# A hybrid attention trunk on one core: the keys of turned weight tiles are written apart by residue modulo four, and values are turned by pairs of columns

## The chip, the cores and the metric

The kernel runs on one core of a Trainium2 chip. The metric is the device time of one execution in microseconds. The engines are named as the profile names them: PE (TensorE: matrix products; PEld is its weight load), ACT (ScalarE), DVE (VectorE), POOL (GpSimd) and SP (SyncE, whose queue issues every DMA of this kernel).

## What is computed

One layer of a streaming encoder on a prompt of 1024 tokens and a sample of 32 tokens, width 1024, with 8 heads of band attention (A) and 8 heads of stick-breaking attention (B), 64 wide each:

```python
qa, ka, va, ga, qb, kb, vb, gb = split(rmsnorm(h, g_pre) @ w_in)     # 8 x 512 columns
# A: each frame sees its own 64-frame chunk and the 8 chunks before
s = qa @ ka.T * 64 ** -0.5 + bias_table[clip(k_pos - q_pos, -128, 128) + 128]
oa = softmax(where(in_band, s, -1e30)) @ va
# B: strictly causal
z = qb @ kb.T * 64 ** -0.5
log_1m = where(causal, log_sigmoid(-z), 0)
after = cumsum(log_1m, reverse=True) - log_1m
ob = where(causal, exp(log_sigmoid(z) + after), 0) @ vb
y = concat(oa * silu(ga), ob * silu(gb)) @ w_out
h = h + rmsnorm(y, g_post)
h = h + sigmoid(h @ w_ple_gate) * (p @ w_ple)
```

Besides the two streams of outputs, the new keys and values of both kinds go out.

## The kernel before

Nothing is issued as it is written. Every call is recorded with its tiles; a planner (`plan`, with the costs of `cost` and the constants at lines 179 to 185) lays the recorded operations out on five engines by list scheduling, sets due times from that layout and lays them out again, three times. The order that comes out is each engine's instruction order, and each engine then runs its own list in order. A change of one cost can therefore move rows on every engine.

The projections run as `col_steps`: for each of 32 groups of 128 columns, three chunks of 352 tokens, 24 products a chunk (`mm_...`), fp32 split into a high and a low part. They are woven with the attention, pair of heads by pair of heads, in the order A0, B0, A1, B1 and so on.

`attention` handles one head. For each block `i` of 128 queries, `scores(i)` makes the scores (`SA`, `SB`), and from them a tile of weights in `be` with 128 queries on the partitions and `n` keys along the row. For A, DVE adds the bias and takes a minimum (`om`, `stat`), and ACT writes the exponential. For B, ACT takes a sigmoid, DVE scans it, and POOL writes the difference of neighbours. Both read `om` (`w0`) and write `be` (`w1`). `weights_t(i)` must bring the keys onto the partitions, since `values(g)` multiplies the weights with the values (`PVA`, `PVB`). It does so in two ways. Small blocks are transposed by PE (`ptw`). The blocks in `ROUND` (A: 4, 5, 6, 7, each alone; B: 4, 5, 6, each alone) are turned without PE: DVE transposes 32 x 32 squares from `be` into `om`, one DMA writes them to a scratch in DRAM (`swap`), a second one reads them back into `be` so that the squares stand on their partitions, ACT casts a high part (`wTh`) and DVE subtracts it for the low part (`wTl`). For the scratch to be written in long runs, a square takes every fourth key: the residue of the key modulo 4 is the slow index.

The values come out of the projection turned the wrong way as well (`st`, 128 features by 1024 tokens). `values_out` transposes them on DVE into `vx`, in squares that take every fourth token, writes them to a scratch with one DMA and reads them back into `st` with another; ACT copies them into `vt`, and they go out and into the operands of the products (`v2`). Keys that go out (`keys_out`, `kt`) are transposed by DVE in plain squares.

All DMAs stand in one SP queue. SP waits, in order, until what a DMA reads is written, so that a DMA that waits holds back all behind it.

Of the kernel before, what the change touches and what calls it, by code (L numbers as in the profile page):

```python
# [10 lines left out]
AF = mybir.ActivationFunctionType  # L11
ALU = mybir.AluOpType

P = 128
D = 1024
# [163 lines left out]
LAND = {"PE": 165, "ACT": 0, "DVE": 0, "POOL": 0, "SP": 0, "CTL": 0}  # L179
SEM = 60  # L180
WAKE = {"PE": 400, "ACT": 100, "DVE": 100, "POOL": 190, "SP": 0}
ISSUE = 520
DMA_RATE, LANDING, WAKE_DMA = 320.0, 2500, 200
TABLE_NS = 1310
DVE_SET, POOL_SET = 137, 110
# [79 lines left out]
class Recorder:  # L265
# [73 lines left out]
    @staticmethod  # L339
    def cost(eng, method, args, kw, writes, reads):  # L340

        out = writes[0] if writes else None
        n = out.free() if isinstance(out, View) else 1
        psum = any(isinstance(v, (View, Segments)) and v.buf.psum for v in reads)
        if eng == "PE":
            if method == "transpose":
                return (109 if args[1].shape[0] > 64 else 62), 165
            return max(109.0, 2.5 + 0.449 * args[2].free()) * (1 if args[2].buf.dtype == F32R else 4), 165
        if eng == "ACT":
            return (90 if psum else 125) + 0.83 * n + (190 if "accum_out" in kw else 0), 105  # L350
        if eng == "DVE":
            if method == "tensor_tensor_scan":
                return 150 + 2.1 * n, 85
            if method == "tensor_copy" and not psum:
                return 100 + 0.53 * n, 85
            if method == "scalar_tensor_tensor":
                return 155 + 1.04 * n, 85
            if method == "tensor_tensor_reduce":
                return 120 + 1.04 * n, 150
            return 100 + 1.04 * n, 85  # L360
        if eng == "POOL":
            if method == "tensor_tensor":
                if n == 1:
                    return 565, 40
                return 200 + (1.77 if out.buf.dtype == F32 else 2.15) * n, 40
            if method == "tensor_scalar":
                return 255 + 0.86 * n, 0
            return 100 + 0.82 * n, 0
        size, run = 4, 0
        for v in (out, args[1]):  # L370
            if isinstance(v, View) and v.buf.pool is not None:
                size, run = 4 * v.shape[0] * v.free(), 4 * v.shape[-1]
        return ISSUE, max(size / DMA_RATE, size / run * (8.5 + 0.0365 * run) / 16)


    def order(self):
# [123 lines left out]
def stream_step(  # L500
# [19 lines left out]
    def scratch(shape, name):  # L520
        return Buf(shape, F32, name=name, real=dram.tile(shape, F32, tag=name, name=name))
# [206 lines left out]
    def values_out(ab, p, src, o_p, o_s, then):  # L728

        h2 = slice(2 * p, 2 * p + 2)  # L730
        b0 = 4 if ab == "A" else 0
        box = {}

        def turn():
            st = src()
            D = scratch([4, P, SEQ // 4], f"swap{ab}{p}")
            x = at2.tile([P, SEQ], F32, tag="tok", name=f"vx{ab}{p}", bufs=2)
            nc.vector.transpose(x.rearrange("p (c b f) -> p b c f", c=4, f=32), st[:, 0:SEQ].rearrange("p (b t c) -> p b c t", c=4, t=32))
            dma(D.rearrange("g (t c) x -> (g t) (c x)", c=4), x)
            dma(st[:, 0:SEQ].rearrange("p (g x) -> p g x", g=4), D.rearrange("g p x -> p g x"))  # L740
            out = at2.tile([P, NT, P], F32, tag="tok", name=f"vt{ab}{p}", bufs=2)
            box["out"] = out
            short_block(st, out, f"ptv{ab}{p}")

        def back():
            out = box["out"]
            nc.scalar.copy(out[:, 0:8, :].rearrange("p b (g f) -> p g b f", g=4), src()[:, 0:SEQ].rearrange("p (g b f) -> p g b f", g=4, f=32))
            dma(o_p[0, 0, :, h2, :].rearrange("(b p) h d -> p b (h d)", p=P), out[:, b0:8, :])
            dma(o_s[0, 0, :, h2, :].rearrange("p h d -> p (h d)"), out[0:NS, 8, :])
            then(out)  # L750

        return [(0.1, turn), (0.0, back)]
# [79 lines left out]
    def attention(ab, p, h):  # L832
# [23 lines left out]
        def rooms(i):  # L856
# [8 lines left out]
            w0, w1 = whole[g]  # L865
            return w0[:, a + more * k:a + more * k + n + more], w1[:, a:a + n]

        def scores(i):
            L, kd, kl = Lq[h], KDh[h], KLD[h]
            b0 = lo_block(i)  # L870
            n = (i + 1 - b0) * P
            k0 = b0 * P
            cut = [0, n] if n <= 512 else [0, n // 2, n]
            w0, w1 = rooms(i)
            pieces = []
            for j in range(len(cut) - 1):
                s = psum("S", f"S{nm}_{i}_{j}")[:, 0:cut[j + 1] - cut[j]]
                lhs = L[:, i * P:(i + 1) * P]
                ks = slice(k0 + cut[j], k0 + cut[j + 1])
                nc.tensor.matmul(s, lhs, kd[:, ks], start=True, stop=False)  # L880
                nc.tensor.matmul(s, lhs, kl[:, ks], start=False, stop=True)
                pieces.append((cut[j], cut[j + 1], s))
            if ab == "B":
                a, b, s = pieces[-1]
                dg = s[:, b - a - P:b - a]
                nc.vector.tensor_tensor(dg, dg, maskb, ALU.add)
                nc.gpsimd.memset(w0[:, n:n + 1], 1.0)
                for a, b, s in pieces:
                    nc.scalar.activation(w0[:, a:b], s, AF.Sigmoid, scale=-1.0)
                for a, b, s in reversed(pieces):  # L890
                    rev = w0[:, a:b][:, ::-1]
                    nc.vector.tensor_tensor_scan(rev, rev, s, w0[:, b:b + 1], ALU.mult, ALU.bypass)
                nc.gpsimd.tensor_tensor(w1[:, 0:n], w0[:, 1:n + 1], w0[:, 0:n], ALU.subtract)
            else:
                m = small.tile([P, 4], F32, tag="stat", name=f"stat{nm}_{i}", bufs=6)
                sums = box["sums"]
                for j, (a, b, s) in enumerate(pieces):
                    nc.vector.tensor_tensor_reduce(
                        w0[:, a:b], s, box["bias"][:, n - b:n - a][:, ::-1], 1.0,
                        3e38 if j == 0 else m[:, j - 1:j], ALU.add, ALU.min, m[:, j:j + 1])  # L900
                last = len(pieces) - 1
                nc.scalar.activation(w1[:, 0:n], w0[:, 0:n], AF.Exp, bias=m[:, last:last + 1], scale=-1.0, accum_out=sums[:, i:i + 1])
                if i == 7:
                    nc.vector.reciprocal(sums, sums)
                    pt = psum("T", f"pts{nm}")
                    nc.tensor.transpose(pt[0:8, 0:P], sums, ident)
                    row = at.tile([P, 4 * P], F32, tag="ot", name=f"sumrow{nm}", bufs=2)[0:8, 0:P]
                    nc.scalar.copy(row, pt[0:8, 0:P])
                    dma(rs_dr[2 * p + h, 0:SEQ].rearrange("(i q) -> i q", q=P), row)
            state[i] = w0, w1  # L910
# [7 lines left out]
        def weights_t(i):  # L918
# [9 lines left out]
            if i in together:  # L928

                group = together[i]  # L930
                done_with.append((i, hi, lo))
                if i != group[-1]:
                    return
                w0, w1 = whole[group]
                m = sum(cost(x) for x in group)
                first = {x: sum(cost(y) for y in group[:k]) for k, x in enumerate(group)}
                squares = w0[:, 0:m * P].rearrange("p (c b q) -> p b c q", c=4, q=32)
                for x, _, _ in done_with:
                    y = slice(first[x], first[x] + cost(x))
                    nc.vector.transpose(squares[:, y], w1[:, y.start * P:y.stop * P].rearrange("p (b k c) -> p b c k", c=4, k=32))  # L940
                dr = scratch([4, P, m * 32], f"swap{nm}_{i}")
                dma(dr.rearrange("g (k c) x -> (g k) (c x)", c=4), w0[:, 0:m * P])
                dma(w1.rearrange("p (g x) -> p g x", g=4), dr.rearrange("g p x -> p g x"))
                turned = w1.rearrange("p (g b q) -> p g b q", g=4, q=32)
                for x, hi, lo in done_with:
                    src = turned[:, :, first[x]:first[x] + cost(x), :]
                    hi, lo = (y.rearrange("p (b g q) -> p g b q", g=4, q=32) for y in (hi, lo))
                    nc.scalar.copy(hi, src)
                    nc.vector.tensor_tensor(lo, src, f(hi), ALU.subtract)
                done_with.clear()  # L950
                return
# [955 lines left out]
```

## Time and profile before

| | |
|---|---|
| median of 3 runs | 796.02 us (794.12 to 798.11) |
| profiled execution | 797.65 us, with a span of 795.9 us in the trace |
| busy over the span | PE 97%, PEld 89%, DVE 78%, ACT 63%, POOL 55% |
| DMA | 177.83 MB, mean 223 GB/s |

Nearly every instruction has the line of the planner's `emit`, L494, so groups are read by tile names: `om<-be` is the turning transposition, `be<-om,statA` the exponential of A, `be<-om` on POOL the difference of B. A group's row has its count, its busy time in us, the mean of one in ns, and the idle time of the engine before it. In the stretches, the clock of 1.00 is TensorE at full speed. PE counts as busy while a product is under way, and products overlap, so short pauses do not show.

### The profile page before, as it was taken

How to read it: one execution, taken by the hardware profiler on the slowest of the kernel's cores; microseconds unless marked ns; L12 is line 12 of the kernel's file. 1: busy time of each engine (PE TensorE's matmuls, PEld its weight loads, DVE VectorE, ACT ScalarE, POOL GpSimd, SP SyncE). 2: the span in 40 equal slices, each digit the busy share in tenths (PEclk: the TensorE clock that was granted, in tenths of full speed). 3: DMA queues.
4: the chain of work that ended last, by engine and by line, in shares of the span. 5: the costliest groups of instructions: out<-in, count | busy, mean ns of one | idle time of the engine just before them, and what ended most of it. 6: DMA issues, size and time to landing. Idle time of an engine off the chain costs nothing.

```text
span 795.9 us, 13838 instructions
## 1 busy us (share of the span) xinstructions
PE 775.4 (97%) x4518; PEld 710.2 (89%) x4518; DVE 622.2 (78%) x1007; ACT 502.9 (63%) x1039; POOL 438.3 (55%) x503
## 2 busy tenths in 40 slices
PE   8999999999999899999999999999999999999997
PEld 7999998999999799999899989999997877888786
DVE  6716799899899789999899799986446778676655
ACT  5736685577686546886567686542349967874841
POOL 4714647773556668145552426867634358596613
PEclk9999999999999999999999999999999999999999
DMA  8519996777998749876446859865679848668634
GB/s 269 162 39 287 286 296 232 210 251 276 274 273 271 208 153 324 232 206 209 122 137 214 206 162 292 264 191 165 196 259 340 288 133 271 225 213 288 252 127 133
DMA packets 175179, 177.83 MB, mean 223 GB/s; under 512 B 38002, under 2 KB 131930, under 8 KB 175107
## 3 DMA queue, kind: packets, MB, share of 16 engines
q1 hardware_dynamic: 175106, 176.95, 72.4%
q8 instruction: 36, 0.59, 0.3%
q14 instruction: 37, 0.30, 0.1%
HBM read 107.62 MB, written 60.88 MB: 212 GB/s over the span
## 4 chain that ended last, share of the span: by engine, by line
PE 41%; DVE 8%; issue 2%; DMA 2%; ACT 1%; POOL 0%; SPq 0%; DVEq 0%; ACTq 0%; POOLq 0%
PE mm_gB L494 6%; PE mm_gA L494 4%; DVE om L494 3%; PE g0P L494 2%; PE o1P L494 2%; PE g1P L494 2%; PE g2P L494 2%; PE o0P L494 2%; PE g3P L494 2%; PE o3P L494 2%; PE o2P L494 2%; PE ple L494 2%; PE PVB L494 2%; PE mm_vA L494 1%; DVE wTl L494 1%
## 5 line engine op out<-in xcount | busy, mean ns | idle before, releaser
L494 POOL TENSOR_TENSOR be<-om 128x384 f32<-128x384 f32 (+7 forms) x64 | 79.4, 1248 | 56.9 <-DVE om L494 19.7
L494 DVE TENSOR_TENSOR_SCAN om<-om,SB 128x384 f32<-128x384 f32 (+5 forms) x96 | 94.6, 998 | 5.5 <-DMA sum_drg<-gB 2.5
L494 DVE STREAM_TRANSPOSE om<-be 128x640 f32<-128x640 f32 (+2 forms) x56 | 79.8, 1433 | 3.8 <-POOL be L494 3.2
L494 DVE TENSOR_TENSOR wTl<-be,wTh 128x640 fp32r<-128x640 f32 (+2 forms) x56 | 58.6, 1050 | 10.3 <-ACT wTh L494 10.1
L494 ACT ACTIVATE om<-SB 128x384 f32<-128x384 f32 (+5 forms) x96 | 44.2, 491 | 32.8 <-DVE SB L494 13.7
L494 ACT CAST wTh<-be 128x640 fp32r<-128x640 f32 (+2 forms) x56 | 43.1, 771 | 17.7 <-DMA be<-swapB 12.5
L494 ACT ACTIVATE be<-om,statA 128x640 f32<-128x640 f32 (+4 forms) x64 | 44.4, 695 | 9.3 <-DVE statA L494 5.1
L494 PE MATMUL SB<-kdB,LB 128*128 128x384 f32 (+5 forms) x96 | 33.7, 354 | 2.3 <-DVE om L494 2.2
L494 POOL TENSOR_TENSOR oB<-oB,oB 128x256 f32<-128x256 f32 x32 | 24.1, 777 | 20.1 <-DMA oB<-in_w_out_dram 19.9
L494 DVE CUSTOM_DVE_ANT_0 om<-SA,biasA 128x320 f32<-128x320 f32 (+3 forms) x64 | 29.8, 482 | 6.8 <-PE SA L494 4.8
L494 ACT CAST wTh<-ptwB 128x512 fp32r<-128x512 f32 (+3 forms) x48 | 22.3, 483 | 17.7 <-PE ptwB L494 11.2
L494 PE MATMUL SB<-klB,LB 128*128 128x384 f32 (+5 forms) x96 | 33.1, 348 | 0.0
L494 POOL TENSOR_TENSOR gB<-gB,gB 128x256 f32<-128x256 f32 x32 | 25.5, 821 | 10.6 <-DMA gB<-in_w_ple_gate_dram 9.1
L494 PE MATMUL SA<-klA,LA 128*128 128x320 f32 (+2 forms) x96 | 29.4, 317 | 0.5 <-DMA klA<-klA 0.5
L494 PE MATMUL SA<-kdA,LA 128*128 128x320 f32 (+2 forms) x96 | 29.5, 317 | 0.3 <-DVE statA L494 0.3
L494 POOL TENSOR_TENSOR sggA<-sggA,oggA 128x352 f32<-128x352 f32 x24 | 23.9, 994 | 7.5 <-DMA oggA<-rs_dr 3.7
L494 POOL TENSOR_TENSOR klB<-stkB,kdB 64x1024 fp32r<-64x1024 f32 x8 | 20.4, 2548 | 13.7 <-ACT kdB L494 9.3
L494 DVE TENSOR_TENSOR wTl<-ptwB,wTh 128x512 fp32r<-128x512 f32 (+3 forms) x48 | 25.4, 542 | 3.1 <-ACT wTh L494 1.6
L494 PE MATMUL PVB<-wTh,v2B 128*128 128x512 f32 (+1 forms) x96 | 22.2, 354 | 3.2 <-ACT wTh L494 2.4
L494 POOL TENSOR_TENSOR h<-h,x 128x512 f32<-128x512 f32 (+1 forms) x18 | 23.9, 1350 | 0.0
L494 PEld LDWEIGHTS PVB<-wTh,v2B 128*128 128x128 f32 x96 | 17.6, 193 | 7.1 <-ACT wTh L494 3.3
L494 POOL TENSOR_TENSOR klA<-stkA,kdA 64x1024 fp32r<-64x1024 f32 x8 | 19.5, 2438 | 7.6 <-ACT kdA L494 7.4
(707 smaller groups left out, 2627.4 us busy)
## 6 DMA issues: line engine op xcount, KB each, us to landing
swapA<-om SPq DMA_DIRECT2D x32, 320.0 KB
be<-swapA SPq DMA_DIRECT2D x32, 320.0 KB
oB<-in_w_out_dram SPq DMA_DIRECT2D x16, 256.0 KB
sum_dro<-oB SPq DMA_DIRECT2D x16, 256.0 KB
gB<-in_w_ple_gate_dram SPq DMA_DIRECT2D x16, 256.0 KB
sum_drg<-gB SPq DMA_DIRECT2D x16, 256.0 KB
x<-in_x_prompt_dram SPq DMA_DIRECT2D x16, 256.0 KB
h_dr<-h SPq DMA_DIRECT2D x8, 512.0 KB
```

Of the source, the lines that this page charges most:

```text
L494: getattr(getattr(tc.nc, o.what[0]), o.what[1])(*args, **kw)
```

## The change

Three edits. First, `apart` gives the round's tiles a permuted view of `be`: ACT's exponential and POOL's difference read `om` in order as before, and write key `4k + c` of each block of 128 to place `32c + k`, that is, neighbouring keys 32 floats (128 bytes) apart. DVE's transposition then reads `be` with unit step. What lies in `om`, in the scratch and after it is the same as before. Blocks that PE transposes are not touched.

Second, the values' squares take every second token instead of every fourth (a step of 8 bytes in place of 16), and the two halves of 512 tokens lie in separate halves of the scratch. The write has two runs of 2 KB for each partition in place of one of 4 KB; the read back is two DMAs of 64 partitions in place of one of 128.

Third, the planner's costs: one issue cost of 520 ns becomes 470, 610 for tiles of 64 partitions, and 660 for views of three dimensions with 16 or more in the middle; and a transposition that reads a view of four dimensions is costed at 1.98 ns an element, a form that no longer occurs with the first two edits (the values' view has five dimensions).

```diff
-ISSUE = 520
+ISSUE, ISSUE_64, ISSUE_SHORT = 470, 610, 660
...
+            if method == "transpose" and len(args[1].shape) == 4:
+                return 1.98 * n + 30, 85
...
+                issue = ISSUE_64 if v.shape[0] == 64 else ISSUE_SHORT if len(v.shape) == 3 and v.shape[1] >= 16 else ISSUE
...
-            D = scratch([4, P, SEQ // 4], f"swap{ab}{p}")
+            D = scratch([2, 4, HD, SEQ // 4], f"swap{ab}{p}")
             x = at2.tile([P, SEQ], F32, tag="tok", name=f"vx{ab}{p}", bufs=2)
-            nc.vector.transpose(x.rearrange("p (c b f) -> p b c f", c=4, f=32), st[:, 0:SEQ].rearrange("p (b t c) -> p b c t", c=4, t=32))
-            dma(D.rearrange("g (t c) x -> (g t) (c x)", c=4), x)
-            dma(st[:, 0:SEQ].rearrange("p (g x) -> p g x", g=4), D.rearrange("g p x -> p g x"))
+            nc.vector.transpose(x.rearrange("p (i j b f) -> p b i j f", i=2, j=2, f=32), st[:, 0:SEQ].rearrange("p (b i t j) -> p b i j t", i=2, t=32, j=2))
+            dma(D.rearrange("i g (t j) x -> (g t) i (j x)", j=2), x.rearrange("p (i x) -> p i x", i=2))
+            for i in range(2):
+                dma(st[HD * i:HD * i + HD, 0:SEQ].rearrange("p (g x) -> p g x", g=4), D[i].rearrange("g p x -> p g x"))
...
+        def apart(i, x, out=False):
+
+            if i not in together:
+                return x
+            return x.rearrange("p (b c k) -> p b k c" if out else "p (b k c) -> p b k c", c=4, k=32)
...
-                nc.gpsimd.tensor_tensor(w1[:, 0:n], w0[:, 1:n + 1], w0[:, 0:n], ALU.subtract)
+                nc.gpsimd.tensor_tensor(apart(i, w1[:, 0:n], True), apart(i, w0[:, 1:n + 1]), apart(i, w0[:, 0:n]), ALU.subtract)
...
-                nc.scalar.activation(w1[:, 0:n], w0[:, 0:n], AF.Exp, bias=m[:, last:last + 1], scale=-1.0, accum_out=sums[:, i:i + 1])
+                nc.scalar.activation(apart(i, w1[:, 0:n], True), apart(i, w0[:, 0:n]), AF.Exp, bias=m[:, last:last + 1], scale=-1.0, accum_out=sums[:, i:i + 1])
...
-                    nc.vector.transpose(squares[:, y], w1[:, y.start * P:y.stop * P].rearrange("p (b k c) -> p b c k", c=4, k=32))
+                    nc.vector.transpose(squares[:, y], w1[:, y.start * P:y.stop * P])
```

The order of rows that the planner makes of it differs on all engines. On SP, the first head's values, before (`stvA0` is read back by one transfer, after the first turned tile's write):

```order
L494 DMA oB110_991<-in_w_out_dram 128x512
L494 DMA klA01_973<-klA01_973 64x1024
L494 DMA swapA00_4_99<-om_189 128x640
L494 DMA stvA0_676<-swapA0_98 128x4x256
L494 DMA out_7_dram<-vtA0_1002 32x128
```

and now:

```order
L497 DMA oB110_981<-in_w_out_dram 128x512
L497 DMA klA01_974<-klA01_974 64x1024
L497 DMA stvA0_676<-swapA0_98 64x4x256 x2
L497 DMA biasA10_1071<-r_dr_76 128x640
L497 DMA swapA00_4_99<-om_189 128x640
```

The read back is two rows of 64 partitions, and it now stands ahead of the first turned tile's write.

More of the change, by code (lines that the diff above doesn't have):

```diff
@@ L368, in cost @@
             return 100 + 0.82 * n, 0
-        size, run = 4, 0
+        size, run, issue = 4, 0, ISSUE
         for v in (out, args[1]):
@@ L372, in cost @@
                 size, run = 4 * v.shape[0] * v.free(), 4 * v.shape[-1]
-        return ISSUE, max(size / DMA_RATE, size / run * (8.5 + 0.0365 * run) / 16)
+                issue = ISSUE_64 if v.shape[0] == 64 else ISSUE_SHORT if len(v.shape) == 3 and v.shape[1] >= 16 else ISSUE
+        return issue, max(size / DMA_RATE, size / run * (8.5 + 0.0365 * run) / 16)
     def order(self):
```

## The prediction

> **What bounds the kernel now.** First the page: the span, and what share of it each engine was busy.
>
> ```profile
> span 795.9 us, 13838 instructions
> PE 775.4 (97%) x4518; PEld 710.2 (89%) x4518; DVE 622.2 (78%) x1007; ACT 502.9 (63%) x1039; POOL 438.3 (55%) x503
> ```
>
> TensorE is busy for 97% of the span, so nothing here can win more than the 20.5 us in which it is not. Where those lie, the busy times by stretch show: the start, the first heads, the attention from 120 to 520 us, the gates, and the two last products. The second fence has the same view in 20 us slices, of which I show five.
>
> ```profile
> 40.00:120.00 80.00, 78.69 (x500) 76.13 (x499) 51.67 (x102) 48.85 (x105) 33.00 (x42) 1.00 0.79 229
> 120.00:520.00 400.00, 389.15 (x2443) 370.51 (x2442) 362.75 (x581) 265.99 (x557) 221.95 (x261) 1.00 0.76 226
> 520.00:600.00 80.00, 80.00 (x504) 78.79 (x503) 45.64 (x73) 30.42 (x63) 48.45 (x51) 1.00 0.63 203
> ```
>
> ```profile
> 140.00:160.00 20.00, 20.00 (x127) 19.22 (x125) 17.61 (x27) 11.42 (x26) 14.95 (x22) 1.00 0.75 211
> 160.00:180.00 20.00, 20.00 (x129) 19.72 (x128) 19.78 (x22) 14.61 (x28) 15.72 (x13) 1.00 0.75 234
> 260.00:280.00 20.00, 17.04 (x96) 15.01 (x94) 15.03 (x20) 11.14 (x25) 13.28 (x18) 0.91 0.72 201
> 280.00:300.00 20.00, 20.00 (x129) 19.10 (x128) 16.60 (x27) 8.59 (x21) 12.98 (x18) 1.00 0.54 171
> 440.00:460.00 20.00, 19.04 (x125) 18.48 (x124) 14.86 (x35) 13.04 (x27) 8.79 (x6) 1.00 0.83 203
> ```
>
> After the length stand the busy times of TensorE, its weight loads, VectorE, ScalarE and GpSimd, then the granted clock. From 40 to 520 us TensorE idles 1.31 + 10.85 = 12.2 us, and 260:280 alone has 3.0 of them and a clock of 0.91 behind them (0.09 x 20 = 1.8 us more). VectorE is the second limit: 362.75 of 400 us, 91%. But a full VectorE is not by itself a waiting TensorE: 160:180 has 19.78 us of VectorE and no idle TensorE, 440:460 has 14.86 and 0.96 us. What TensorE waits for is local, and the view of waits for 40 to 520 us names it:
>
> ```profile
> PE PVB L494 <- ACT wTh L494: 2.4, 3, 1.1
> PE SB L494 <- DVE om L494: 2.2, 4, 0.9
> PE ptksB L494 <- DMA be<-in_cache_b_k_dram: 1.0, 1, 1.0
> PE PVA L494 <- ACT wTh L494: 1.0, 1, 1.0
> PE PVB L494 <- DVE v2B L494: 0.8, 1, 0.8
> PE ptsA L494 <- DVE sumsA L494: 0.8, 2, 0.6
> PE ptwB L494 <- POOL be L494: 0.8, 1, 0.8
> PE ptsA L494 <- DVE wTl L494: 0.6, 1, 0.6
> PE PVA L494 <- DVE otA L494: 0.5, 1, 0.5
> ```
>
> The columns are total us, times, longest. Waits on VectorE make 2.2 + 0.8 + 0.8 + 0.6 + 0.5 = 4.9 us here, waits on the ScalarE cast of weights that come back turned (wTh) 3.4 us. About 9 us hang on the chain that the change touches: weights, VectorE's turn, two transfers, cast, product.
>
> **The change part by part.** The turn itself. VectorE's transpositions stand in the groups by shape, among them two that read unit steps already (kt, the keys that go out):
>
> ```profile
> L494 DVE STREAM_TRANSPOSE om<-be 128x640 f32<-128x640 f32 x40 | 52.7, 1329 | 0.9 <-ACT be L494 0.4 <-POOL be L494 0.3
> L494 DVE STREAM_TRANSPOSE om<-be 128x896 f32<-128x896 f32 x8 | 14.5, 1809 | 1.8 <-POOL be L494 1.8
> L494 DVE STREAM_TRANSPOSE om<-be 128x768 f32<-128x768 f32 x8 | 12.6, 1573 | 1.1 <-POOL be L494 1.0
> L494 DVE STREAM_TRANSPOSE vxB<-stvB 128x1024 f32<-128x1024 f32 x4 | 8.2, 2047 | 0.9 <-ACT stvB L494 0.9
> L494 DVE STREAM_TRANSPOSE vxA<-stvA 128x1024 f32<-128x1024 f32 x4 | 8.2, 2044 | 0.6 <-ACT stvA L494 0.6
> L494 DVE STREAM_TRANSPOSE ktB<-stkB 128x1024 f32<-128x1024 f32 x4 | 5.0, 1239 | 0.0
> L494 DVE STREAM_TRANSPOSE ktA<-stkA 128x512 f32<-128x512 f32 x4 | 2.8, 694 | 11.4 <-ACT stkA L494 11.4
> ```
>
> At one size, 1024, every fourth float costs 2046 ns and unit step 1239. Unit step is (1239 - 694)/512 = 1.064 ns an element on 149: 830 ns at 640, 966 at 768, 1102 at 896. The turned tiles now read unit step, so 40 x 499 + 8 x 607 + 8 x 707 = 30.5 us leave VectorE. The values read every second float: no row has that; it lies between the two rows of 1024, so 8 x 0 to 8 x 807 ns = 6.5 us. I take 6.5. [...]
>
> Together 37 us of VectorE. If all fell in 120:520, its 91% there would become 81%.
>
> What is added: the same keys are written 128 bytes apart, by 32 exponentials of ScalarE and 24 differences of GpSimd.
>
> ```profile
> L494 ACT ACTIVATE be<-om,statA 128x640 f32<-128x640 f32 x32 | 26.6, 831 | 2.8 <-DVE statA L494 1.2 <-PE ptwA L494 1.1 <-DVE wTl L494 0.4
> L494 ACT CAST wTh<-be 128x640 fp32r<-128x640 f32 x40 | 28.9, 726 | 6.7 <-DMA be<-swapB 3.4 <-DMA be<-swapA 2.8
> L494 ACT CAST kdA<-stkA 64x1024 fp32r<-64x1024 f32 x8 | 8.4, 1048 | 3.2 <-PE SB L494 3.2
> L494 ACT CAST oB<-raw 128x512 fp32r<-128x512 f32 x4 | 2.4, 621 | 0.0
> L494 POOL TENSOR_TENSOR be<-om 128x640 f32<-128x640 f32 x8 | 11.3, 1408 | 11.6 <-ACT stvA L494 2.6 <-DVE om L494 2.5 <-ACT om L494 2.3
> L494 POOL TENSOR_TENSOR be<-om 128x768 f32<-128x768 f32 x8 | 13.5, 1687 | 7.1 <-ACT otA L494 3.8 <-DVE om L494 1.1 <-DVE be L494 1.1
> L494 POOL TENSOR_TENSOR be<-om 128x896 f32<-128x896 f32 x8 | 14.2, 1769 | 11.6 <-DVE om L494 6.1 <-ACT stvA L494 3.8 <-PE ptksB L494 0.8
> ```
>
> No row writes single floats apart. Low end: ScalarE's cast wTh reads and writes runs of 32 floats, and its 726 ns lie on the line through the two plain casts (621 + 128 x 0.834 = 728), so a stride costs it nothing; less than nothing is excluded, since the elements are the same number. High end: VectorE's ratio, 2046/1239 = 1.65, gives ScalarE 0.65 x 26.6 = 17.3 us, and GpSimd 0.65 x (11.3 + 13.5 + 14.2) = 25.4. I take nothing for ScalarE, whose own row is nearest, and nothing for GpSimd, whose 2.0 to 2.2 ns an element (1408/640, 1769/896) are more than twice the 0.83 of ScalarE's line, so that one write may hide behind two reads. Even the high ends load them to (266 + 17)/400 = 71% and (222 + 25)/400 = 62%; what they would cost is delay in the chain, below.
>
> The values' swap: the write goes out as two runs a row instead of one, and the read back as two transfers of 64 rows.
>
> ```profile
> L494 SPq DMA_DIRECT2D stvA<-swapA x4: 371/622/1547, 76.6 to 420.4; - x4
> L494 ACT COPY vtA<-stvA x4: 1040/1046/1052, 85.8 to 426.7; 128x1024 f32<-128x1024 f32 x4
> L494 ACT COPY vtB<-stvB 128x1024 f32<-128x1024 f32 x4 | 4.2, 1050 | 3.8 <-DMA stvB<-swapB 3.8
> L494 SPq DMA_DIRECT2D kdA<-kdA x8: 482/482/1217, 59.4 to 411.1; - x8
> SPq L494 <- DVE om L494: 47.5, 33, 7.0
> ```
>
> Eight more issues at 0.48 (kdA, also 64 rows) to 0.62 us are 4 to 5 us of SP's queue, 0.5 each time; behind them stand weight loads and the turned tiles' writes. The last row says that SP itself stood 47.5 us, 33 times, before VectorE's turned tiles: a turn shorter by 0.5 to 0.7 us gives that back, 56 times. I cost the extra issues at nothing: the first values of A are copied 9 us after their read is issued, the last 6; for B ScalarE waited 3.8 us in all while TensorE had other products queued. Without that cover they cost 0.5 x 8 = 4 us.
>
> The planner's new issue costs move rows everywhere. VectorE at the end of head A00, names as in the kernel (statA01 is the next head's first minimum): before,
>
> ```order
> L494 STREAM_TRANSPOSE om_189<-be_203 128x5x4x32
> L494 TENSOR_TENSOR wTl_180<-ptwA00_2_0_1025,wTh_531 128x384
> L494 RECIPROCAL sumsA00_230<-sumsA00_230 128x8
> L494 STREAM_TRANSPOSE om_189<-be_203 128x5x4x32
> L494 TENSOR_TENSOR wTl_180<-ptwA00_3_0_1072,wTh_531 128x512
> L494 STREAM_TRANSPOSE om_189<-be_203 128x5x4x32
> L494 ISA om_189,statA01_0_961<-SA01_0_0_1034,biasA01_385 128x128
> ```
>
> and now:
>
> ```order
> L497 STREAM_TRANSPOSE om_189<-be_203 128x5x4x32
> L497 TENSOR_TENSOR wTl_180<-ptwA00_2_0_988,wTh_531 128x384
> L497 TENSOR_TENSOR wTl_180<-ptwA00_3_0_1030,wTh_531 128x512
> L497 RECIPROCAL sumsA00_230<-sumsA00_230 128x8
> L497 STREAM_TRANSPOSE om_189<-be_203 128x5x4x32 x3
> L497 STREAM_TRANSPOSE ktB0_1057<-stkB0_1028 128x1024
> L497 ISA om_189,statA01_0_964<-SA01_0_0_1046,biasA01_385 128x128
> ```
>
> The turns are bunched, and with the keys' one 3 x 0.83 + 1.24 = 3.7 us stand ahead of A01's first minimum. TensorE's row for that head's values, just where the turned tiles are first used (mm_vB0 is projection work): before,
>
> ```order
> L494 MATMUL mm_vB0_0_1304<-hnl0_167,wh_vB0_0_1122 128x352 x4
> L494 MATMUL mm_vB0_0_1304<-hnl0_167,wh_vB0_1_1130 128x352
> L494 MATMUL PVA00_1_1281<-wTh_531,v2A00_677 128x512
> L494 MATMUL PVA00_1_1281<-wTh_531,v2A00_677 128x384
> L494 MATMUL PVA00_1_1281<-wTh_531,v2A00_677 128x256
> ```
>
> and now:
>
> ```order
> L497 MATMUL ptwA01_3_0_1336<-ident_170,be_203 128x128 x4
> L497 MATMUL mm_vB0_0_1309<-hnh0_164,wl_vB0_0_1098 128x352
> L497 MATMUL PVA00_1_1258<-wTh_531,v2A00_677 128x512
> L497 MATMUL PVA00_1_1258<-wTh_531,v2A00_677 128x384
> L497 MATMUL PVA00_1_1258<-wTh_531,v2A00_677 128x256
> ```
>
> The product has moved up past ten projection matmuls, 1.6 us at 80 us for 500 in the 40:120 row.
>
> The sum. Of the 9 us that hang on the chain, each single wait is 0.5 to 1.1 us, and a turn gives back 0.5 to 0.7: half go, 4.5 us. With the pauses the clock dip goes mostly, 1.5. Together 6 us. The profiled execution took 797.65, 1.6 above the median of 796.02; I lay the sum on the median: 790.0.
>
> **The rivals.**
> Full relief: all 9 us, the dip and the rest of the chain's small ones, 12 in all: 784. Against it: every in-order row has some wait.
>
> The stride only changes engine. At 1.65, the exponential is 0.54 us and the difference 0.92 to 1.15 us longer, so a turned tile is no earlier; only VectorE's 4.9 us of waits shrink, by half: 793.5. For it speaks that VectorE's own row shows the price. [...]
>
> Waits are local and new ones replace them: 796.
>
> Slower: the new order puts products ahead of their tiles. Place: PVA00_1 and its like in all 16 heads; price: a wait of 0.9 us (the mean of the four on wTh, 3.4/4) in each is 14.4 us, less 6: 804.4. It decides from about seven heads on (6/0.9). For it: the product moved up 1.6 us, one turn gives 0.5. Against: three bunched turns give 1.5.
>
> **How the numbers follow.** About 0.5%, 4 us, is what a measurement of this kernel can tell from no change. Forecast 0.44 (nine tenths of it under 792), full relief 0.10 (all faster), the stride moved 0.15 (a fifth faster, else same), replaced waits 0.09 (same), slower order 0.22 (nine tenths over 800). Faster 0.396 + 0.10 + 0.03 = 0.53; same 0.044 + 0.12 + 0.09 + 0.02 = 0.27; slower 0.20. The range runs from 782, just beyond full relief, to 805, the slower order.
>
> **What would show it.** Right: turned transpositions at 830, 966 and 1102 ns, values near 1239, VectorE near 585 us busy, ScalarE's exponential at 831 and GpSimd's rows unchanged, TensorE's waits on wTh halved. Wrong: an exponential near 1370 ns; idle TensorE from 40 to 520 us above 12.2; waits of PVA and PVB on wTh in many heads.

## The result: no change, and the profile after

The changed kernel takes 796.01 us (median of 20 runs, 792.99 to 800.32), the one before, beside it, 795.26 (20 runs, 792.03 to 798.77): a ratio of 1.0012, interval 0.9995 to 1.0030. I had forecast 790.0. The profiled execution took 796.99 us. The page of the changed kernel:

```profile
span 795.2 us, 13848 instructions
PE 772.9 (97%) x4518; PEld 709.4 (89%) x4518; DVE 600.3 (75%) x1007; ACT 519.7 (65%) x1039; POOL 447.9 (56%) x503
```

VectorE lost 21.9 us of busy time, ScalarE gained 16.8 and GpSimd 9.6. The stretches, with the columns as before:

```profile
40.00:120.00 80.00, 76.85 (x486) 73.86 (x485) 47.35 (x98) 51.59 (x102) 31.62 (x40) 1.00 0.79 217
120.00:520.00 400.00, 389.88 (x2456) 373.30 (x2455) 343.77 (x581) 278.14 (x556) 231.80 (x264) 1.00 0.78 227
```

From 40 to 520 us TensorE idles 3.15 + 10.12 = 13.3 us, against 12.2: the prediction had named more than 12.2 as the sign that it is wrong. The groups by shape say which of its prices:

```profile
L497 ACT ACTIVATE be<-om,statA 128x640 f32<-128x640 f32 x32 | 46.1, 1481 | 1.1 <-PE ptwA L497 1.1
L497 DVE STREAM_TRANSPOSE om<-be 128x640 f32<-128x640 f32 x40 | 33.0, 829 | 8.9 <-ACT be L497 8.0 <-POOL be L497 0.8
L497 DVE STREAM_TRANSPOSE om<-be 128x896 f32<-128x896 f32 x8 | 8.8, 1105 | 1.5 <-POOL be L497 1.2 <-POOL om L497 0.3
L497 DVE STREAM_TRANSPOSE om<-be 128x768 f32<-128x768 f32 x8 | 7.7, 966 | 1.0 <-POOL om L497 0.9
L497 DVE STREAM_TRANSPOSE vxB<-stvB 128x1024 f32<-128x1024 f32 x4 | 4.9, 1235 | 0.1
L497 POOL TENSOR_TENSOR be<-om 128x896 f32<-128x896 f32 x8 | 15.6, 1944 | 9.7 <-ACT om L497 2.4 <-DMA swapB<-om 2.1 <-DVE newl L497 1.9
L497 POOL TENSOR_TENSOR be<-om 128x768 f32<-128x768 f32 x8 | 14.0, 1751 | 8.8 <-ACT v2B L497 4.8 <-ACT otB L497 4.1
L497 POOL TENSOR_TENSOR be<-om 128x640 f32<-128x640 f32 x8 | 12.2, 1530 | 7.0 <-DVE om L497 3.1 <-ACT wTh L497 2.3 <-DVE wTl L497 1.6
```

The transpositions have the predicted durations. The exponential went from 831 to 1481 ns: 650 ns more on ScalarE for 500 less on VectorE, for the same tile. The end of the second row is as telling: VectorE stood 0.4 us before the exponential's tile in the kernel before, and stands 8.0 us now. GpSimd's rows are 64 to 175 ns a tile longer than before, and 146 to 214 longer than in the same order with plain writes (1384, 1581 and 1730 ns in the rest alone, below). TensorE's waits from 40 to 520 us:

```profile
PE ptsA L497 <- DVE sumsA L497: 5.2, 7, 1.5
PE PVB L497 <- DVE otA L497: 1.9, 1, 1.9
PE ptkB L497 <- ACT stkB L497: 1.1, 1, 1.1
PE PVB L497 <- ACT wTh L497: 0.9, 1, 0.9
...
PE PVA L497 <- ACT wTh L497: 0.6, 2, 0.3
```

The waits on the cast (wTh) fell from 3.4 to 1.5 us. In their place stands the product that transposes A's sums (ptsA): 0.8 us before, 5.2 now. The exponential accumulates those sums, so they end as late as it does. Part of this wait belongs to the new order: the rest alone, below, has 2.2 us of it with a plain exponential.

### The profile page after: what moved, and what is told of

It reads as the page before. It is cut to its first block, busy times and chain, and to the rows that moved or that the text cites. A ratio compares the mean times of both kernels' runs of the same rounds, so it can differ in the third digit from the quotient of the medians.

```text
span 795.2 us, 13848 instructions
## 1 busy us (share of the span) xinstructions
PE 772.9 (97%) x4518; PEld 709.4 (89%) x4518; DVE 600.3 (75%) x1007; ACT 519.7 (65%) x1039; POOL 447.9 (56%) x503
## 5 line engine op out<-in xcount | busy, mean ns | idle before, releaser
L497 POOL TENSOR_TENSOR be<-om 128x128 f32<-128x128 f32 (+7 forms) x64 | 84.0, 1324 | 57.2 <-DVE om L497 10.5
L497 ACT ACTIVATE be<-om,statA 128x640 f32<-128x640 f32 (+4 forms) x64 | 63.9, 1021 | 9.6 <-DVE wTl L497 4.2
L497 DVE TENSOR_TENSOR wTl<-be,wTh 128x640 fp32r<-128x640 f32 (+2 forms) x56 | 62.2, 1115 | 10.6 <-ACT wTh L497 10.4
L497 DVE STREAM_TRANSPOSE om<-be 128x640 f32<-128x640 f32 (+2 forms) x56 | 49.6, 888 | 11.4 <-ACT be L497 8.0
L497 POOL TENSOR_TENSOR oB<-oB,oB 128x256 f32<-128x256 f32 x32 | 26.8, 862 | 15.0 <-DMA oB<-in_w_out_dram 14.8
L497 DVE CUSTOM_DVE_ANT_0 om<-SA,biasA 128x320 f32<-128x320 f32 (+2 forms) x64 | 29.7, 482 | 7.0 <-PE SA L497 5.2
L497 POOL TENSOR_TENSOR gB<-gB,gB 128x256 f32<-128x256 f32 x32 | 28.3, 902 | 11.9 <-DMA gB<-in_w_ple_gate_dram 10.8
L497 POOL TENSOR_TENSOR sggA<-sggA,oggA 128x352 f32<-128x352 f32 x24 | 25.7, 1075 | 6.4 <-DVE sggA L497 2.3
L497 POOL TENSOR_TENSOR sggB<-sggB,oggB 128x352 f32<-128x352 f32 x12 | 11.9, 988 | 20.3 <-DVE sggB L497 15.7
```

The source lines that it names most:

```text
L497: getattr(getattr(tc.nc, o.what[0]), o.what[1])(*args, **kw)
```

## The experiments

Theory 1: the step went from VectorE's reads (16 bytes) to ScalarE's writes (128 bytes), and costs more there. Theory 2: the turn's relief was there, and the new order of rows (with the values and the issue costs) lost it. Theory 3: TensorE's waits are mostly local, so that no relief of VectorE is worth much. A ratio is to the kernel before, run beside it, with its 95% interval. "In the order before" means that only views change, and each engine keeps its rows as in the kernel before. That kernel took 796.07 us beside the parts and the rest, 797.81 beside the issue costs, the turn taken away, the pairs and the planner told, 797.41 beside VectorE in ScalarE's place, the halves and the halves in the changed kernel, and 796.86 beside the last two.

**The parts alone.** Only A's tiles apart, in the order before:

```diff
-nc.scalar.activation(w1[:, 0:n], w0[:, 0:n], AF.Exp, ...)
+nc.scalar.activation(apart(i, w1[:, 0:n], True), apart(i, w0[:, 0:n]), AF.Exp, ...)
...
+nc.vector.transpose(squares[:, y], src if ab == "A" else src.rearrange("p (b k c) -> p b c k", c=4, k=32))
```

> The kernel before with only ScalarE's exponential of the A tiles written apart and their 32 transpositions read with unit step; GpSimd, values and issue costs as before, and every engine's row order is that of before, so only durations differ. Theory 1 (the stride has only changed engine for A: exponential 1481 in place of 831 ns, transposition 829 in place of 1329): a turned A tile is 0.15 us later, TensorE waits on sumsA grow from 0.8 us to about 5, the time is 795 to 798, same or up to 3 us slower. Theory 2 (the durations won some 6 us and the new order lost them): 791 to 793. Theory 3 (TensorE's waits are local, whatever the chain costs): 795 to 796.

Measured: 799.63 us, ratio 1.0038 (1.0017 to 1.0059): slower, with 13.9 us less on VectorE (608.3).

Only B's tiles apart, by GpSimd, with the same edit for B:

> The kernel before with only GpSimd's difference of the B tiles written apart and their 24 transpositions read with unit step; the row order is that of before. Theory 1 (GpSimd pays nothing, so B is the half that gains): transpositions 830, 966, 1105 ns, 15 us less of VectorE, GpSimd's rows of 640 to 896 within 0.1 us of 1408, 1687, 1769, waits of PVB on wTh below 2.4 us, time 791 to 794. Theory 2: 793 to 794, a share of the same gain. Theory 3: 795 to 796.

Measured: 795.18, ratio 0.9984 (0.9962 to 1.0007): no gain that can be told, with 9.2 us less on VectorE (613.0), where theory 1 had 791 to 794. Both, in the order before:

> The kernel before with both kinds of tiles written apart, values and issue costs as before, and the row order of before. Theory 1 (A loses what B gains): 793 to 797, VectorE about 592 us, ScalarE about 523. Theory 2 (the new order is what lost the gain): 789 to 791. Theory 3: 795 to 796.

Measured: 796.64, ratio 0.9999 (0.9975 to 1.0023). Its exponential, its turn and its wait of ptsA, with which the runs in halves are compared below:

```profile
L494 ACT ACTIVATE be<-om,statA 128x640 f32<-128x640 f32 x32 | 46.9, 1496 | 1.1 <-PE ptwA L494 1.1
L494 DVE STREAM_TRANSPOSE om<-be 128x640 f32<-128x640 f32 x40 | 32.6, 825 | 5.6 <-ACT be L494 4.5 <-POOL be L494 0.9
```

```profile
PE ptsA L494 <- DVE sumsA L494: 1.9, 4, 1.0
```

The first edit brings nothing in the old order either, so it isn't the new order that took its gain. The rest alone, in the changed kernel's order, with the values by pairs and the new issue costs, and nothing written apart:

```diff
 def apart(i, x, out=False):
...
-nc.scalar.activation(apart(i, w1[:, 0:n], True), apart(i, w0[:, 0:n]), AF.Exp, ...)
+nc.scalar.activation(w1[:, 0:n], w0[:, 0:n], AF.Exp, ...)
```

> The changed kernel without the first edit: nothing is written apart, the turned tiles are read at every fourth float as before (829 back to 1329 ns, exponential back to 831), but the values by pairs, the new issue costs and the row order of the changed kernel stay. Theory 1 (the order is worth about nothing): 795 to 798. Theory 2 (the order loses what the durations won): 800 to 803. Theory 3: 795 to 797.

Measured: 798.34, ratio 1.0025 (1.0000 to 1.0050). Its exponential takes 826 ns, and still:

```profile
PE ptsA L495 <- DVE sumsA L495: 2.2, 4, 0.6
```

And the issue costs alone, whose order of rows is a third one:

```diff
-ISSUE = 520
+ISSUE, ISSUE_64, ISSUE_SHORT = 470, 610, 660
```

> The kernel before with the third edit alone, the planner's new issue costs; only the row order differs. x_rest, which has this, the values by pairs and the order of the changed kernel, was 0.25% slower than before. If the order is what costs that: 797 to 799. If the values' second read is: 795 to 796.

Measured: 799.27, ratio 1.0010 (0.9979 to 1.0041). By the interval of the rest alone, the other edits cost 0 to 0.5%, not the six us that theory 2 needs. The values by pairs were not run alone.

**The turn taken away**, in the order before:

```diff
-nc.vector.transpose(squares[:, y], src)
+nc.vector.transpose(squares[:, y][:, 0:1, 0:1], src[:, 0:1, 0:1])
```

> The kernel before, in its row order, with each of the 56 turning transpositions cut to one block of 32 columns (about 0.15 us each), so the weights that come back are not turned ones, and with the mask's constant at -3e4 in place of -1e30. It leaves out all of what the turn costs VectorE, some 70 us, and nothing is added on ScalarE or GpSimd: the upper bound of what a faster turn can bring in this order. Theory 1 (the chain limits, and the gain of the changed kernel went to ScalarE's stride): 12 us of idle TensorE shrink by more than half, 786 to 789. Theory 3 (TensorE's waits are local and mostly not this chain's): 792 to 795.

Measured: 792.06, ratio 0.9929 (0.9900 to 0.9958). The group and the stretches of this run:

```profile
L494 DVE STREAM_TRANSPOSE om<-be 128x32 f32<-128x32 f32 x56 | 11.8, 218 | 3.6 <-POOL be L494 1.8 <-ACT be L494 0.7 <-DMA out_dram<-vtA 0.7
```

```profile
40.00:120.00 80.00, 79.85 (x512) 77.91 (x511) 45.32 (x102) 50.93 (x109) 35.23 (x43) 1.00 0.81 235
120.00:520.00 400.00, 393.80 (x2490) 378.56 (x2489) 315.67 (x589) 267.05 (x559) 227.52 (x268) 1.00 0.78 229
```

68 us less in the turn's rows (52.7 + 14.5 + 12.6 - 11.8; VectorE's busy time falls by 62.4) are worth 5.6, and 0.15 + 6.2 us of TensorE's idle time remain. At this point I read it as a rate, 0.08 us for each us; the runs in halves below show that this was wrong.

**Other ways to spare the step.** A's tiles turned by pairs, as the change does with the values (two DMAs of 64 rows for each read back; on the changed kernel, the exponential plain):

```diff
+nc.vector.transpose(squares[:, y], src.rearrange("p (b i t j) -> p b i j t", i=2, t=32, j=2) if pairs else src)
...
+for z in range(2):
+    dma(w1[HD * z:HD * z + HD].rearrange("p (g x) -> p g x", g=4), dr[z].rearrange("g p x -> p g x"))
```

> The changed kernel with the A tiles turned as it turns the values: ScalarE writes the exponential plainly, VectorE reads every second float, the scratch has two halves and the read back is two transfers of 64 rows (32 more issues on SP); the B tiles stay written apart by GpSimd. Theory 1: exponential 831 ns, transposition 830, TensorE waits on sumsA below 2 us, time 791 to 794, below the changed kernel by 2 to 4. Theory 3: 795 to 797. Theory 4 (SP's queue has no room): over 798, with ScalarE waiting longer for what comes back.

Measured: 809.33, ratio 1.0140 (1.0099 to 1.0181). Exponential 830 ns and turn 824, both as short as plain ones (831 and 829), and yet the slowest of all these kernels: the DMAs of this kernel, and what ScalarE's casts then wait for:

```profile
be<-swapA SPq DMA_DIRECT2D x64, 160.0 KB, 3.9
```

```profile
ACT wTh L497 <- DMA be<-swapB: 18.6, 13, 3.6
ACT wTh L497 <- DMA be<-swapA: 11.3, 14, 1.9
```

In the changed kernel the same two waits are:

```profile
ACT wTh L497 <- DMA be<-swapB: 7.0, 6, 3.1
...
ACT wTh L497 <- DMA be<-swapA: 5.6, 8, 1.1
```

Theory 4 had forecast this slower time and these longer waits. That 32 more issues on SP's queue are its cause is not shown, though: the planner made another order of rows of this kernel, with 14 loads of ScalarE's function tables (ACT_TABLE_LOAD) in place of 12, at 1283 ns each, and one of the fastest kernels below (the halves in the changed kernel) has 13.8 and 7.1 us of the same two waits. The changed kernel, with the planner told the exponential's true duration:

```diff
+slow = 1.02 * n if "accum_out" in kw and len(out.shape) == 4 else 0
-return (90 if psum else 125) + 0.83 * n + (190 if "accum_out" in kw else 0), 105
+return (90 if psum else 125) + 0.83 * n + slow + (190 if "accum_out" in kw else 0), 105
```

> The changed kernel with its planner told that an exponential written apart costs 1.02 ns an element more (the measured 1481 against 831 ns); nothing else differs but the row order that follows. Theory 1, in the form that TensorE waits for sumsA because the plan has the exponential 0.65 us early: waits on sumsA fall from 5.2 to below 2 us and the time to 791 to 794. Theory 3: other waits take their place, 795 to 797.

Measured: 802.57, ratio 1.0066 (1.0039 to 1.0093). Of its waits, one of TensorE's and one of ScalarE's:

```profile
PE ptsA L498 <- DVE sumsA L498: 0.9, 1, 0.9
```

```profile
ACT wTh L498 <- DMA be<-swapB: 23.8, 13, 5.9
```

The wait of ptsA is nearly gone, but the casts now wait 23.8 us for B's read backs, and the new order also has four more loads of ScalarE's tables:

```profile
L498 ACT ACT_TABLE_LOAD x16 | 20.5, 1283 | 1.3 <-PEq L1906 0.7 <-DVE statA L498 0.3
```

The order that this planner made for the longer exponential is worse; whether the waits or the loads make it so was not tried.

VectorE writing apart in ScalarE's place, in the order before (its minimum writes each key a quarter of the tile away from the one before; GpSimd as in the change):

```diff
-w0[:, a:b], s, ...
+w0[:, 0:n].rearrange("p (c k) -> p k c", c=4)[:, a // 4:b // 4], s.rearrange("p (k c) -> p k c", c=4), ...
```

> The kernel before, row for row, with both kinds of tiles apart, but for A VectorE writes apart: its minimum of scores and bias writes each key a quarter of the tile away from the one before, the exponential is plain, and the turned tiles read unit step. If VectorE's writes pay as ScalarE's do, the minimum (484 and 544 ns at 320) rises by 200 to 330 ns each, 64 of them 13 to 21 us, against 16 us taken from the turn: 796 to 798. If its writes are free as GpSimd's nearly are, the minimum stays at 484 to 544, VectorE loses 26 to 30 us with nothing added to ScalarE and the time is 793 to 795. The rival of local waits: the same as before, 796, either way.

Measured: 793.61, ratio 0.9946 (0.9919 to 0.9974). Its minimum by shape:

```profile
L494 DVE CUSTOM_DVE_ANT_0 om<-SA,biasA,statA 128x320 f32<-128x320 f32 x32 | 25.7, 809 | 1.9 <-PE SA L494 0.9
L494 DVE CUSTOM_DVE_ANT_0 om<-SA,biasA 128x320 f32<-128x320 f32 x32 | 23.7, 754 | 2.0 <-DMA swapA<-om 1.6 <-PE SA L494 0.2
```

544 and 484 ns became 809 and 754: VectorE's writes pay too, as the first case said, but the time is the second case's. VectorE still ends 13.8 us below before (608.4), ScalarE as it was, and that is worth 0.5%. So theory 3 does not hold either: this much relief is worth something, as long as ScalarE doesn't pay for it. With ScalarE paying (A alone, 608.3) the kernel was slower.

**In halves.** The exponential reads pairs of neighbouring floats 16 bytes apart and writes runs of 64; the turn then reads every second float. GpSimd as in the change, all in the order before:

```diff
+w1x = w1x.rearrange("p (b d k e) -> p d b k e", d=2, k=32, e=2)
+w0x = w0x.rearrange("p (b k d e) -> p d b k e", d=2, k=32, e=2)
+nc.scalar.activation(w1x, w0x, AF.Exp, ...)
...
+src = src.rearrange("p (b d k e) -> p b d e k", d=2, k=32, e=2)
+nc.vector.transpose(w0[:, 0:m * P].rearrange("p (d e b q) -> p b d e q", d=2, e=2, q=32)[:, y], src)
```

> The kernel before, row for row, with both kinds of tiles apart, but the A tiles in two halves of the price: the exponential reads pairs of neighbouring floats 16 bytes apart and writes runs of 64, and VectorE's turn then reads every second float. GpSimd writes the B tiles apart as in the change. Theory 1 (a step is paid where a 16-byte stretch holds one float of the access, on ScalarE's writes as on VectorE's reads): with two floats in each stretch neither pays; exponential 831 to 900 ns against 1481 in the changed kernel, turned tiles of 640 at 830, so VectorE is some 26 to 30 us shorter with nothing added to ScalarE; by the rate of the run without the turn (5.6 us for some 70 of VectorE) that is 2 to 2.5 us: 793 to 795 beside 796 to 797. Rival (TensorE's waits have nothing to do with the turned tiles' delay): within 0.5 us of the kernel before. If the exponential stays near 1480, the price hangs on the step and not on how much of a stretch is used.

Measured: 789.32 us, ratio 0.9902 (0.9865 to 0.9939). Its groups:

```profile
L494 DVE STREAM_TRANSPOSE om<-be 128x640 f32<-128x640 f32 x40 | 32.6, 824 | 2.7 <-POOL be L494 1.3 <-ACT be L494 1.2
L494 ACT ACTIVATE be<-om,statA 128x640 f32<-128x640 f32 x32 | 28.1, 880 | 2.2 <-PE ptwA L494 1.1 <-DVE statA L494 0.7 <-DVE wTl L494 0.4
```

Hardly anything is paid now: the turn has its 824 ns, the exponential 49 ns more than the plain one, and VectorE's wait on it is 1.2 us, where the same order with single floats (both, above) had 4.5. The order and the turn's duration are the same in these two runs, and so is GpSimd's edit; an exponential of 880 in place of 1496 ns makes 0.9902 out of 0.9999. The exponential of 640 keys takes 1481 ns where it writes single floats 128 bytes apart (1496 in both, above), 880 where it reads pairs 16 bytes apart, 897 where it writes pairs apart (below), and 831 plain.

The halves' stretches, and behind them the kernel before's first 40 us, which the prediction does not show:

```profile
0.00:40.00 40.00, 38.25 (x218) 33.67 (x219) 29.00 (x48) 25.94 (x51) 24.32 (x47) 1.00 0.69 215
40.00:120.00 80.00, 78.71 (x502) 76.78 (x502) 50.36 (x100) 49.78 (x106) 35.21 (x43) 1.00 0.82 235
120.00:520.00 400.00, 392.51 (x2485) 376.33 (x2484) 343.05 (x590) 269.30 (x560) 231.22 (x266) 1.00 0.78 229
```

```profile
0.00:40.00 40.00, 37.46 (x205) 33.09 (x206) 28.07 (x46) 25.20 (x49) 24.32 (x47) 1.00 0.70 215
```

Products count progress better than idle time does, here of one execution each. The counts of the stretches up to 520 us add up to 3205 here and 3148 before; 42 of those 57 come from 120 to 520 us, 13 from the start, which the edit hardly touches. From 120 to 520 us idle time fell only 10.85 - 7.49 = 3.4 us, while 42 products at 392.51/2485 = 0.158 us are 6.6. Part of the other half is the clock. Where the kernel before had 0.91 (260:280, in the prediction), the halves have 1.00:

```profile
260.00:280.00 20.00, 18.09 (x109) 15.98 (x108) 15.32 (x22) 11.64 (x27) 15.87 (x21) 1.00 0.69 208
```

The halves run 3.9 us ahead with the product that the kernel before starts at 276.5 us, as its clock has just dropped to half (0.50 from 276.5 to 279.7 us), and 5.1 us ahead with the one that it starts at 279.7 us, when the clock is back (1.00 from 280 to 291 us): 1.2 us. The remaining 2 us fit pauses too short to show as idle, which no view here shows by themselves.

The same with the other side of the exponential broken (it reads in order and writes pairs into two halves), for its duration:

```diff
-w1x = w1x.rearrange("p (b d k e) -> p d b k e", d=2, k=32, e=2)
+w1x = w1x.rearrange("p (d b k e) -> p (b k) d e", d=2, k=32, e=2)
```

> As the run in halves, but the exponential reads every float in turn and writes pairs apart: it writes floats alternately into two halves of the tile, two neighbouring keys to either, in runs that are broken after every second float. The columns of A's weights are left in the wrong places; this run is for the duration of the exponential alone. Theory 1 as a rule on 16-byte stretches: 831 to 900 ns if a write is charged for each return to a stretch, 1480 if each jump between halves costs as a single float apart does, near 1150 if a jump costs for each pair. Turned tiles of 640 stay at 830.

```profile
L494 ACT ACTIVATE be<-om,statA 128x640 f32<-128x640 f32 x32 | 28.5, 897 | 1.6 <-PE ptwA L494 1.1 <-DVE statA L494 0.4
```

Pairs are written at 897 ns (one run, 789.08 us): the jump after every second float costs 66 ns a tile, a float by itself 650.

The halves put into the changed kernel, with its order, values and issue costs:

> The changed kernel with the exponential in halves (pairs read 16 bytes apart, runs of 64 written; the turn reads every second float), all else, its rows too, as in the change. If ScalarE's price is what the change's gain went into: exponential 831 to 900 ns, the wait of the sums' product on VectorE's sums back from 5.2 to about 1 us, and 793 to 794.5, 2 to 3 below the changed kernel. If the changed order and issues hold the time: 796, no better than the changed kernel.

Measured: 790.32, ratio 0.9906 (0.9870 to 0.9941); exponential 878 ns, and no wait of ptsA on the sums among TensorE's. With the views of the exponential and of A's turn changed, the whole change has its forecast gain: 790.0/796.02 is 0.9924, which lies in the interval. Both runs in halves beat the kernel before and the changed one.

The same time put on ScalarE without a scattered write: the halves, in the same order, with a plain copy ahead of each of the 32 exponentials:

```diff
+tc.nc.scalar.copy(w1x[:, :, 0:4], w0x[:, :, 0:4])
 nc.scalar.activation(w1x, w0x, AF.Exp, ...)
```

> The run in halves (x_split: 789.3, exponential 880 ns), row for row, with one row more ahead of each of the 32 exponentials of turned A tiles: a plain ScalarE copy of 512 of the tile's floats into the place that the exponential then overwrites, about 621 to 660 ns, so 20 to 21 us more on ScalarE and each tile 0.6 us later, with no float written by itself. If the change's gain went into ScalarE's time (the exponential's 650 ns more), this brings it back: 795 to 798. If it went into what scattered writes do to the other engines at the memory, the time stays at 789 to 791.

Measured: 801.44, ratio 1.0085 (1.0055 to 1.0115).

```profile
L496 DVE STREAM_TRANSPOSE om<-be 128x640 f32<-128x640 f32 x40 | 32.6, 826 | 7.3 <-ACT be L496 6.6 <-POOL be L496 0.6
L494 ACT COPY be<-om 128x512 f32<-128x512 f32 x32 | 21.0, 658 | 0.3 <-DVE statA L496 0.2
```

```profile
PE ptsA L496 <- DVE sumsA L496: 5.0, 5, 1.6
```

Both signs of the changed kernel are back: VectorE waits 6.6 us for the exponential, and ptsA 5.0 us for the sums. So time on ScalarE, with no float written by itself, is enough to undo the gain. The copy is no exact stand-in, though: single floats had 4.5 and 1.9 us of these waits in the same order (both, above) and a ratio of 0.9999. That the copy costs more than they do and than the forecast of 795 to 798 (14.6 us for 21.0) isn't explained by these runs. The rival, that scattered writes slow the other engines at the memory, shows in none of three rows compared between single floats and halves: VectorE's minimum with statA 546 and 545 ns, its wTl 907 and 977, GpSimd's difference of 896 keys 1969 and 1974.

The halves for A alone, B as before:

> The run in halves for the A tiles alone; the B tiles are written and turned as in the kernel before, row for row in its order. VectorE is 32 x 0.5 = 16 us shorter, ScalarE 1.6 longer, and the B tiles' turn costs what it did. If the two kinds' gains add up, 0.9902 less the 0.0016 that B alone gave: ratio near 0.992, 791. If the gain needs both, 793 to 796.

Measured: 793.74, ratio 0.9964 (0.9930 to 0.9999). A's part alone gives 0.4%, B's 0.2%, both 1.0%. That both give more than their sum can't be told within these intervals.

## Why the prediction was wrong

**The step that failed** is the price of ScalarE's writes: "I take nothing for ScalarE, whose own row is nearest". That row, the cast, moves runs of 32 floats (726 ns, 728 on the line of the plain casts); the exponential writes single ones (1481 ns, 831 plain). The run of 32 said nothing on a float alone, and pairs show that a jump by itself wasn't the price: with one after every second float the exponential takes 880 ns (reading) and 897 (writing), 49 and 66 more than plain, where single floats took 650 more. (On ScalarE only neighbouring pairs were tried; VectorE reads every second float in 824 ns, and unit step in 829.) Even the high end was short: I priced 17.3 us by VectorE's ratio of 1.65, and 32 x 650 ns are 20.8, a ratio of 1.78.

**The rival that came true** is "The stride only changes engine", which had a chance of 0.15: 500 ns left VectorE's turn of 640 and 650 came onto ScalarE's exponential. It was priced too well: "a turned tile is no earlier" became 0.15 us later, and in place of 793.5 the gain was nil. The sums that the exponential accumulates came later as well, which the rival did not have: ptsA waits 5.2 us for them, against 0.8 before and 2.2 in the same order with a plain exponential.

**The sum of gains** came out, in part by luck: "half go, 4.5 us", and 1.5 of the clock dip, with ScalarE at nothing, is a ratio of 0.9924; with ScalarE at 49 ns a tile the two runs in halves measure 0.9902 and 0.9906, with intervals that hold it. That half of the waits go was a guess that no run tests by itself, and that the clock dip goes with the pauses was an estimate from one stretch of before, which the runs don't show as a rule: 260:280 has 1.00 with 0.05 us of idle TensorE in the changed kernel, 1.91 in the halves and 2.79 in both (above), where before had 0.91 with 2.96; and the changed kernel has its own dip of 0.91 at 480:500, with 1.93. In the execution in halves 3.4 us of idle time went from 120 to 520 us and 1.2 us of the clock dip; the other 2 us were in no term of the sum. Nor does the gain grow with the relief: the whole turn taken away gives 0.9929, no more than the halves, and why isn't shown.

**VectorE's 37 us** were right as removed rows, 19.7 + 4.9 + 5.7 for tiles and 6.6 for values (no row of before shows the 6.5, the upper end of 0 to 6.5; the changed kernel's rows of 1234 and 1235 ns do), but "VectorE near 585 us busy" was not: it is 600.3. In the changed order other rows of VectorE got longer:

```profile
L497 DVE TENSOR_TENSOR wTl<-be,wTh 128x640 fp32r<-128x640 f32 x40 | 41.6, 1045 | 3.5 <-ACT wTh L497 3.3
```

This was 975 ns before, 1109 in the run of the rest alone and 1089 with the issue costs alone, so the order does it and not the writing apart. The row makes 2.9 of the 15 us, and two rows of newl<-vnsA,newh, 0.4 us each before and 1.7 and 2.6 now, another 3.5; the rest lies in many small ones. What in the order does it wasn't tried.

**GpSimd at nothing** was near: 64 to 175 ns a tile, 2.9 us in 24 differences (146 to 214 ns and 4.2 us beside the rest alone, in the same order), against the high end of 25.4.

**The extra issues at nothing** held for the values' eight: the halves in the changed kernel have them and are no slower than the halves in the old order (0.9906 and 0.9902). What 32 more cost by themselves isn't shown.

**The slower order** (0.22) did not come: the rest alone takes 1.0025, not 804.4, and in the changed kernel PVA and PVB wait for wTh 1.5 us in all.

## What to carry to other kernels

Before a stride is moved to another engine, find a row of that engine that touches single floats as the new code will; a row of runs did not price it here (the cast's 726 ns lie on the plain casts' line, 728; the exponential went from 831 to 1481). Where both sides of a permutation pay, try to split it between them: here ScalarE reading pairs (878 ns in place of 1481) and VectorE reading every second float (827) were the difference between nothing and 1% (0.9906, 0.9870 to 0.9941). And an engine at 65% busy can still be the wrong one to load, when what it writes is the next step's only input: VectorE stood 8.0 us before the exponential's tile, 0.4 before.

## What the runs showed of the hardware

A float moved by itself costs, over a plain access: VectorE reading every fourth (1329 - 829)/640 = 0.78 ns an element, VectorE writing each a quarter of the tile from the one before (809 - 544)/320 = 0.83, ScalarE writing 128 bytes apart (1481 - 831)/640 = 1.02, and GpSimd, its writes alone 128 bytes apart, (1751 - 1687)/768 = 0.08 to (1944 - 1730)/896 = 0.24, with two reads an element beside it. In pairs ScalarE pays 49/640 = 0.08, reading them 16 bytes apart, and (897 - 831)/640 = 0.10, writing them into two halves, and VectorE, reading every second float, nothing that shows (824 ns beside 829, and 1235 beside 1239 at 1024).
